# Where the tiles of a one-core decoder step lie in SBUF: normalised inputs every 2304 bytes, gated outputs every 2112, two places for raw weights

## The chip, the core and the metric

The program runs on one core of one Trainium2 chip. Five engines work side by side, each through a list of its own: TensorE (PE) multiplies, VectorE (DVE), ScalarE (ACT) and GpSimd (POOL) work element by element, and SyncE (SP) issues the DMAs. The metric is the device time of the whole program in microseconds, the median of several runs.

## What is computed

One step of a small decoder with two layers, for a prompt of 512 tokens and 8 single sample tokens; the 520 columns are kept side by side.

```python
def trunk(x, p, pos, hgrn_state, k_past, v_past, ...):
    for l in range(DEPTH):                      # DEPTH = 2
        xn = rmsnorm(h, pre_norm_g[l])
        if l < N_A_LAYERS:                      # layer 0: HGRN2
            mix, S = hgrn2_mixer(xn, w_in_a[l], lb_all[l], onorm_a[l], w_out_a[l], S0)
        else:                                   # layer 1: sliding-window attention with sinks
            kv = rmsnorm(h, kv_norm_g) @ w_kv
            ...
            u = xn @ w_in_b[j]
            q, z = jnp.split(u, 2, axis=-1)
            ...
            mix = (o.reshape(B, L, MIX_WIDTH) * jax.nn.silu(z)) @ w_out_b[j]
        h = h + rmsnorm(mix, post_norm_g[l])
        h = h + (p[l] @ w_pe[l]) * jax.nn.sigmoid(h @ w_pg[l])
```

Model width 1024, mixer width 2048, 16 heads of 128 in layer 0, 32 query heads of 64 over 4 key heads in layer 1, a window of 128. Everything is float32.

## The kernel before, in words

**Products in three passes.** Each float32 operand of a projection is split into a high and a low part that TensorE takes as fp32r. A product is hi·hi + lo·hi + hi·lo: `mm` (line 597) issues, for one weight chunk of 128 x 128 and one input tile, wh with x's high part, wl with x's high part, and wh with x's low part. Each pass is made for both halves of the 520 columns, 260 wide (`half_of`, line 411), so six matmuls of 260 columns for a chunk. Stages that are worked in halves of the sequence (`end_of`, line 419: the residual, the gates, the last output product) use 256 and 264 columns instead, from columns 0 and 256. The halves of one output go to a pair of PSUM banks, `pj`, of which there are two; other work uses single banks, `ph`.

**Weights.** `piece` (line 564) loads a weight tile of 128 x 1024 (512 KB) from HBM into one of three places `wr`. `halves` (line 585) makes from each half of it, a piece of 512 columns, the high part `wh` with an ACT cast and the low part `wl` with a subtraction on DVE or POOL. There are four places (`SPLITS`) for `wh` and four for `wl`, and every second pair of the gates' weights uses four pieces of the shared tag `b4`. A piece serves four chunks, 24 matmuls. `stream` (line 533) walks over all output tiles of the kernel in order and asks for a piece as soon as the one four pieces earlier has had its last use.

**Tiles of activations.** `act` (line 437) takes a place of 128 partitions by 520 float32 columns, 2080 bytes in each partition, from a pool in which each tag has a fixed number of places one behind the other. The tags lie in the order tmp, g, x, acc, og, xr, R, xs, behind the constants and the pool of wr, wh and wl; further pools follow behind xs. `xs_` (line 449) hands out the sixteen places of normalised inputs: high and low parts of eight row blocks, the moving operand of nearly all projections, and the gated outputs of the last heads. `og_` (line 452) hands out twelve places: the gated outputs of the other heads, which the output product reads, and before and between the layers some inputs and residuals.

**Order.** Nothing is issued where it is written. Each call is entered into a `Plan` with its dependencies; `issue` (line 209) then goes through a model of the engines, with a price for each instruction and a number of free places for each tag, and gives each engine its order. Where a tile's place isn't free in the model, its first writer isn't chosen; a DMA stands in SP's list by the same rule. SP's list is one queue for all DMAs: weights, states, turns of tiles through DRAM (`td`), results. At run time each engine keeps to its order and waits for semaphores.

**Stages.** Up to about 40 us the start: embedding products and the first head's projections from unnormalised inputs in og and xr. Then 15 more heads of layer 0, each with four projections of eight chunks, with the heads' own work beside them, and output products in groups. From about 570 to 635 us the second half of layer 0 (residual, gates). Then keys and values, eight units of layer 1 with four projections each, and from about 1010 us the last residual and gates.

All instructions are issued by one helper, so each has line 171 in the profile; the groups are told apart by their tiles' names.

Of the kernel before, what the change touches and what calls it, by code (L numbers as in the profile page):

```python
# [9 lines left out]
F32 = mybir.dt.float32  # L10
# [8 lines left out]
P = 128  # L19
D_MODEL = 1024  # L20
KC = D_MODEL // P
SEQ = 512
NB = 8
T = SEQ + NB
# [34 lines left out]
IDLE, SLOW = 3.4, 6.8  # L59

WINDOW, LOADS = 1600, 700

KEEP = {"tmp": 2, "g": 8, "xr": 4}

# [301 lines left out]
def bank_of(ps, h):  # L366
    return ps[h] if isinstance(ps, list) else ps[:, h]


def chunks_of(loads, n):  # L370

    ws = [Weights(loads[j]) for j in range(n)]
    return [(ws[m * n // KC], m * n % KC) for m in range(KC)]
# [45 lines left out]
def end_of(x, half):  # L419
    return x[:, ENDS[half][0] : sum(ENDS[half])]  # L420


class Step:
# [13 lines left out]
    def act(self, tag, bufs, dtype=F32, cols=T):  # L437
        return self.plan.tile(self.ap, [P, cols], dtype, self.name(tag), tag, bufs)

    def x_(self, dtype=F32):  # L440
        return self.act("x", 8, dtype)

# [4 lines left out]
        return self.act("g", 15, dtype, cols)  # L447

    def xs_(self, dtype=F32R):
        return self.act("xs", 16, dtype)  # L450

    def og_(self, dtype=F32R):
        return self.act("og", 12, dtype)

    def tmp_(self, dtype=F32, cols=T):
        return self.act("tmp", 4, dtype, cols)
# [107 lines left out]
    def piece(self, order, n):  # L564
        w, half = order[n]
        if half in w.pieces:
            return
        if w.raw is None or n < 2:

            cols = [half] if n < 2 else [h for h in range(2) if (w, h) in order]  # L570
            w.raw = self.plan.tile(self.wp, [P, KC * P], F32, self.name("wr"), "wr", 3)
            sl = slice(cols[0] * PIECE, (cols[-1] + 1) * PIECE)
            self.nc.sync.dma_start(w.raw[:, sl], w.src[:, sl])
        w.pieces[half] = self.halves(w.raw[:, half * PIECE : (half + 1) * PIECE], w.spare)
# [174 lines left out]
    def out_tiles(self, src, n, parts, before, mix, first, after=None):  # L749

        nc = self.nc
        xs = []

        def start():
            assert before()
            if not xs:
                xs.extend(parts())

        def evac(m):
            def f(ps):  # L760
                if first:
                    mix[m] = self.x_()
                    nc.scalar.copy(self.two(mix[m]), self.flat(ps))
                else:
                    nc.vector.tensor_tensor(self.two(mix[m]), self.two(mix[m]), self.flat(ps), op=ALU.add)

            return f

        def evac_half(q, half):
            def f(ps):  # L770
                for a in range(2):
                    m = 2 * q + a
                    x = end_of(mix[m], half)
                    nc.vector.tensor_tensor(x, x, bank_of(ps, a)[:, : ENDS[half][1]], op=ALU.add)
                    if m == 0 and half == 0:
                        self.acc = self.act("acc", 1)
                    self.square_into(end_of(self.acc, half), x, m == 0)
                if m == KC - 1:
                    after(half)

            return f

        at = chunks_of(src, n)
        if after is None:
            return [Tile128([at[m]], n, xs, evac(m), start) for m in range(KC)]
        return [
            Tile128(at[2 * q : 2 * q + 2], n, xs, evac_half(q, half), start, half)
            for half in range(2)
            for q in range(KC // 2)
        ]  # L790
# [615 lines left out]
    def pre_norm(self, xs, gain, raw, Rs, out):  # L1406

        nc = self.nc
        acc = self.act("acc", 1)
        for c in range(KC):  # L1410
            self.square_into(acc, xs[c], c == 0)
            g = self.vec[:, gain + c : gain + c + 1]
            hi, lo = self.og_(), self.og_() if c < 4 else self.xr_(F32R)
            nc.scalar.activation(hi, xs[c], AF.Copy, scale=g)
            nc.vector.scalar_tensor_tensor(lo, xs[c], g, hi.bitcast(F32), op0=ALU.mult, op1=ALU.subtract)
            raw.append((hi, lo))
        R = self.act("R", 1)
        for half in range(2):
            self.rstd(acc, half, R)
        Rs.append(R)  # L1420
        for c in range(KC):
            nc.vector.scalar_tensor_tensor(
                xs[c], xs[c], self.vec[:, gain + c : gain + c + 1], R, op0=ALU.mult, op1=ALU.mult
            )
            out.append(self.split(xs[c], self.xs_))
# [23 lines left out]
    def run(self):  # L1449
# [78 lines left out]
        def finish0(m, half, h):  # L1528
            if half == 0:
                if m == 0:  # L1530
                    self.acc1 = self.act("acc", 1)

                    both = self.small("m", [P, 2, T], 1)
                    self.C, self.S = both[:, 0], both[:, 1]
                    for t, src in ((self.C, "ropeC"), (self.S, "ropeS")):
                        nc.sync.dma_start(t, i[src])
                kvx.append((self.g_(F32R), self.og_()))
            self.beside(lambda: parts(m, half, h), SIDE if half == 0 and m < 4 else MAIN)

        def parts(m, half, h):  # L1540
            nc.sync.dma_start(end_of(hd[m], half), h)
            g = self.vec[:, KVG + m : KVG + m + 1]
            hi, lo = (end_of(x, half) for x in kvx[m])
            nc.scalar.activation(hi, h, AF.Copy, scale=g)
            nc.vector.scalar_tensor_tensor(lo, h, g, hi.bitcast(F32), op0=ALU.mult, op1=ALU.subtract)
            self.square_into(end_of(self.acc1, half), h, m == 0)
            if m == KC - 1:
                self.beside(lambda: self.kv_norm(half, h1, qx), FIRST)

        tiles += in_turn(end + self.gates(0, h1, h1x, pe[0], kept[0], finish0))  # L1550


# [182 lines left out]
```

## Time and profile before

| | us |
|---|---|
| median of 3 runs | 1081.44 |
| lowest and highest run | 1079.11, 1082.64 |
| span of the profiled execution, first to last instruction | 1076.6 |
| mean time between the span and the median of the runs | 4.8 |

The 4.8 us are the difference of two different executions; the profiled one's own time outside its span isn't shown. The memory traffic of the whole span is moderate, and the shortest transfers are the many of turned tiles:

```profile
HBM read 134.16 MB, written 31.97 MB: 154 GB/s over the span
```

In the rows of groups, the first number behind the bar is the group's busy time in us, the second the mean time of one instruction in ns, and then comes the idle time of the engine just ahead of them and who ended it. In rows of a timeline the first number is the start and the second how long the merged instructions took, both in us.

### The profile page before, as it was taken

The numbers are of one execution on the slowest core, as the hardware profiler recorded it, in microseconds if no ns is written. First come the engines' busy times: TensorE is split into PE (matmuls) and PEld (weight loads), VectorE is DVE, ScalarE is ACT, GpSimd is POOL, SyncE is SP. The second block draws the span as 40 slices with busy tenths as digits, with TensorE's granted clock in tenths as the row PEclk, the third lists the DMA queues.
The fourth block names the chain that finished last, engine by engine and source line by source line (L and its number), as shares of the span: only waits on it lengthen the run. The fifth ranks groups of instructions, "written<-read, shape, count | busy, mean of one in ns | idle before, by whom it ended". The sixth has DMA issues, their size and how long they took to land.

```text
span 1076.6 us, 24015 instructions
## 1 busy us (share of the span) xinstructions
PE 1064.7 (99%) x8876; PEld 1056.3 (98%) x8876; DVE 916.3 (85%) x1974; ACT 688.0 (64%) x1829; POOL 116.3 (11%) x196
## 2 busy tenths in 40 slices
PE   9999999999999999999999999999999999999998
PEld 8999999999999999999999999999999999999998
DVE  8897888884878968888889999799998988889984
ACT  7787777755777637767736565477677664665542
POOL 1121122101111012011110000000100001010000
PEclk9999999999999999999999999999999999999999
DMA  8455566655755657576654455644434253424432
GB/s 318 156 192 191 149 192 211 208 175 159 224 164 165 198 143 226 174 218 197 192 170 143 143 189 143 167 132 124 127 100 126 81 153 99 133 93 138 140 99 80
DMA packets 134397, 173.22 MB, mean 161 GB/s; under 512 B 69892, under 2 KB 88268, under 8 KB 134280
## 3 DMA queue, kind: packets, MB, share of 16 engines
q1 hardware_dynamic: 134280, 171.69, 52.1%
q8 instruction: 70, 1.15, 0.5%
q14 instruction: 47, 0.39, 0.1%
HBM read 134.16 MB, written 31.97 MB: 154 GB/s over the span
## 4 chain that ended last, share of the span: by engine, by line
PE 90%; DVE 4%; ACT 3%; issue 2%; DMA 1%; SPq 0%; POOL 0%; POOLq 0%; DVEq 0%; ACTq 0%
PE pj L171 69%; PE ph L171 21%; DMA xr<-td 1%; DVE tmp L171 1%; DVE wl L171 1%; DVE g L171 1%; ACT g L171 0%; ACT tmp L171 0%; ACT wh L171 0%; DVE x L171 0%; DVE xr L171 0%; ACT L171 0%; DVE xs L171 0%; SPq L171 0%; ACT sb L171 0%
## 5 line engine op out<-in xcount | busy, mean ns | idle before, releaser
L171 PE MATMUL pj<-xs,wh 128*128 128x260 f32 (+2 forms) x3264 | 558.7, 285 | 2.4 <-ACT xs L171 1.8
L171 PEld LDWEIGHTS pj<-xs,wh 128*128 128x128 f32 x3264 | 459.0, 188 | 4.3 <-ACT xs L171 3.0
L171 PE MATMUL pj<-xs,wl 128*128 128x260 f32 (+2 forms) x1632 | 338.8, 285 | 0.0
L171 PEld LDWEIGHTS pj<-xs,wl 128*128 128x128 f32 x1632 | 254.3, 188 | 0.2
L171 ACT CAST wh<-wr 128x512 fp32r<-128x512 f32 x288 | 177.5, 620 | 104.9 <-PE pj L171 90.8
L171 DVE TENSOR_TENSOR wl<-wr,wh 128x512 fp32r<-128x512 f32 x273 | 187.7, 690 | 44.2 <-ACT wh L171 40.6
L171 PE MATMUL pj<-og,wh 128*128 128x260 f32 x1056 | 183.3, 285 | 0.0
L171 PEld LDWEIGHTS pj<-og,wh 128*128 128x128 f32 x1056 | 149.7, 188 | 0.4 <-DVE g L171 0.2
L171 PE MATMUL pj<-og,wl 128*128 128x260 f32 x512 | 107.1, 286 | 0.0
L171 PEld LDWEIGHTS pj<-og,wl 128*128 128x128 f32 x512 | 80.1, 188 | 0.0
L171 ACT ACTIVATE tmp<-pj 128x520 f32<-128x520 f32 (+2 forms) x78 | 42.5, 556 | 49.8 <-PE pj L171 49.5
L171 ACT ACTIVATE sb<-sb,g 128x128 f32<-128x128 f32 x128 | 64.7, 560 | 5.1 <-DVE sb L171 5.1
L171 ACT ACTIVATE sb<-sb,nv 128x128 f32<-128x128 f32 x128 | 64.5, 565 | 0.4
L171 ACT COPY b<-ph 128x256 f32<-128x256 f32 (+1 forms) x80 | 27.7, 351 | 44.6 <-PE ph L171 44.1
L171 ACT ACTIVATE b<-b,an 128x129 f32<-128x129 f32 x128 | 50.7, 399 | 5.5 <-DVE an L171 4.5
L171 ACT COPY b<-g 128x256 f32<-128x256 f32 (+1 forms) x112 | 40.8, 375 | 20.7 <-DVE g L171 15.8
L171 PE MATMUL ph<-xs,b 128*128 128x256 f32 (+1 forms) x360 | 50.9, 283 | 0.0
L171 DVE TENSOR_TENSOR x<-x,pj 128x520 f32<-128x520 f32 (+2 forms) x64 | 39.6, 624 | 12.7 <-PE pj L171 12.3
L171 DVE COPY_PREDICATED xr<-lmask,ph 128x256 f32<-128x256 int32 x96 | 46.8, 489 | 3.3 <-PE ph L171 2.7
L171 PE MATMUL ph<-xr,b 128*128 128x128 f32 x320 | 49.1, 275 | 0.0
L171 DVE TENSOR_TENSOR g<-g,b 128x256 f32<-128x256 f32 x96 | 41.1, 429 | 8.1 <-PE ph L171 4.9
L171 PEld LDWEIGHTS ph<-xs,b 128*128 128x128 f32 x360 | 46.4, 188 | 0.1
(214 smaller groups left out, 1746.2 us busy)
## 6 DMA issues: line engine op xcount, KB each, us to landing
wr<-in_w_in_a SPq DMA_DIRECT2D x64, 512.0 KB, 4.8
sb<-sd SPq DMA_DIRECT2D x32, 512.0 KB, 4.7
wr<-in_w_in_b SPq DMA_DIRECT2D x32, 512.0 KB, 3.9
td<-tmp SPq DMA_DIRECT2D x42, 256.0 KB, 3.0
xr<-td SPq DMA_DIRECT2D x168, 64.0 KB, 3.6
sb<-in_state SPq DMA_DIRECT2D x16, 512.0 KB, 5.9
out_st_s<-sb SPq DMA_DIRECT2D x16, 512.0 KB, 2.9
wr<-in_w_out_a SPq DMA_DIRECT2D x16, 512.0 KB, 4.9
```

The costliest lines, as they stand in the source:

```text
L171: op = Op(len(self.ops), self.level, on, [lambda c=c: c(*a, **k) for c in calls], [self.price(e, name, ins, a, k) for e in on], on[0] == " ...
```

## The change

The sixteen xs places become 576 columns (2304 bytes) wide and the twelve og places 528 (2112 bytes); both hand out the 520 columns that begin four columns (16 bytes) into the place. The single place `acc` becomes 528 columns wide, of which the first 520 are used. Raw weights have two places `wr` instead of three. No instruction is added or removed, and no operand changes its shape.

```diff
+INSET, OG_COLS, XS_COLS = 4, T + 8, T + 56
...
+    def inset(self, tag, bufs, dtype, cols):
+
+        return self.act(tag, bufs, dtype, cols)[:, INSET : INSET + T]
+
...
     def xs_(self, dtype=F32R):
-        return self.act("xs", 16, dtype)
+        return self.inset("xs", 16, dtype, XS_COLS)

     def og_(self, dtype=F32R):
-        return self.act("og", 12, dtype)
+        return self.inset("og", 12, dtype, OG_COLS)
...
-            w.raw = self.plan.tile(self.wp, [P, KC * P], F32, self.name("wr"), "wr", 3)
+            w.raw = self.plan.tile(self.wp, [P, KC * P], F32, self.name("wr"), "wr", 2)
...
-                        self.acc = self.act("acc", 1)
+                        self.acc = self.act("acc", 1, cols=OG_COLS)[:, :T]
```

The same edit of `acc` stands in `pre_norm` (line 1409) and in `finish0` (line 1531). T is 520, P 128 and KC 8.

More of the change, by code (lines that the diff above doesn't have):

```diff
@@ L1408, in pre_norm @@
         nc = self.nc
-        acc = self.act("acc", 1)
+        acc = self.act("acc", 1, cols=OG_COLS)[:, :T]
         for c in range(KC):
@@ L1530, in finish0 @@
                 if m == 0:
-                    self.acc1 = self.act("acc", 1)
+                    self.acc1 = self.act("acc", 1, cols=OG_COLS)[:, :T]
                     both = self.small("m", [P, 2, T], 1)
```

## The prediction

> **What bounds the kernel now.** I read the page's table of busy times first, then its slices, then the chain of work that ended last, and last the groups kept apart by shape.
>
> ```profile
> PE 1064.7 (99%) x8876; PEld 1056.3 (98%) x8876; DVE 916.3 (85%) x1974; ACT 688.0 (64%) x1829; POOL 116.3 (11%) x196
> PEclk9999999999999999999999999999999999999999
> PE 90%; DVE 4%; ACT 3%; issue 2%; DMA 1%; SPq 0%; POOL 0%; POOLq 0%; DVEq 0%; ACTq 0%
> PE pj L171 69%; PE ph L171 21%; DMA xr<-td 1%; DVE tmp L171 1%; DVE wl L171 1%; DVE g L171 1%; ACT g L171 0%; ACT tmp L171 0%; ACT wh L171 0%; DVE x L171 0%; DVE xr L171 0%; ACT L171 0%; DVE xs L171 0%; SPq L171 0%; ACT sb L171 0%
> L171 PE MATMUL pj<-xs,wh 128*128 128x260 f32 x2944 | 500.2, 285 | 0.7 <-DVE xs L171 0.4 <-ACT xs L171 0.2
> L171 PE MATMUL pj<-xs,wl 128*128 128x260 f32 x1472 | 306.0, 285 | 0.0
> L171 PE MATMUL pj<-og,wh 128*128 128x260 f32 x1056 | 183.3, 285 | 0.0
> L171 PE MATMUL pj<-og,wl 128*128 128x260 f32 x512 | 107.1, 286 | 0.0
> ```
>
> TensorE is busy for 1064.7 of 1076.6 us at its full granted clock, and 90% of the chain is matmuls. Hardly anything ever waits in front of PE: 0.7 us of idle time stand before the 2944 commonest matmuls. So the kernel lasts as long as its list of matmuls, and only two things move the end much: how far apart consecutive matmuls start, or new gaps in the list.
>
> The mean of 285 ns is the time from a matmul's start to its end. Several are in flight, so it is not the pace. The pace is the distance from start to start. It can be read in the chain in order of time, where one unbroken run of projections stands:
>
> ```profile
> 657.81 33.86 PE pj L171 x283
> ```
>
> 33.86 us over 283 matmuls is 119.6 ns each. Multiplied by the 8876 records, 120 ns gives 1065 us, the busy time. The 260-wide products of xs (2944 + 1472 = 4416) and og (1056 + 512 = 1568) are two thirds of the list.
>
> **The pace and where an operand begins.** The change alters no instruction on PE; it alters the byte at which the moving operand begins. The program of before puts its first xs place at byte 153312 of a partition, which is 224 modulo 256, and the places are 2080 bytes (520 columns of four) apart. 2080 is 32 more than a multiple of 256, so the sixteen places go through all eight multiples of 32. A projection reads the second half at column 260, 1040 bytes on, 16 more modulo 256. The weight pieces wh and wl all begin at 160 modulo 256, before and after.
>
> I took the distance from each 260-wide xs matmul to the next 260-wide one, leaving out distances over 140 ns (gaps and changes of type), and sorted them by the starting byte modulo 256. The first and the last rows of the 4416:
>
> ```profile
> 41.44 0.41 PE L171 MATMUL pj<-xs,wh 128*128 128x260 f32 x2
> ...
> 961.78 0.40 PE L171 MATMUL pj<-xs,wh 128*128 128x260 f32 x2
> ```
>
> 4037 distances are left, with a mean of 119.8 ns. Two of the sixteen starts stand out: 144 (202 distances) with 117.9 ns and 160 (300) with 117.7 ns, each uncertain by 0.2. The other fourteen lie between 119.3 and 121.0, the slowest being 0, 64, 176 and 192 with 120.8 to 121.0. On og, whose places have other addresses, 144 gives 118.9 and 160 gives 118.3 against a mean of 119.8. So this isn't one tile's accident: the same two residues are quick in tiles far apart.
>
> The Trainium skill, "TensorE: Matmul & The Clock Gate", section "Wait — 56ns, not 53.3ns?", puts a warm matmul at its columns over 2.4 GHz plus about 2.5 ns; that would be 110.8 ns for 260 columns. The trace has 119.8, so some 9 ns of each matmul are not in that rule, which is room for a loss that depends on addresses.
>
> **The change part by part.**
>
> *xs places at 144.* Taking a wr place away moves what follows by −4096; the longer acc adds 32 and the longer og twelve times 32. 153312 − 4096 + 32 + 384 = 149632, which is 128 modulo 256, and four columns of inset make it 144. At a distance of 2304 = 9 × 256 all sixteen start at 144, so their second halves start at 160. The pace becomes (117.9 + 117.7) / 2 = 117.8 ns instead of 119.8: 2.0 ns by 4416 is **−8.7 us**. From below, nothing is gained if the two are quick for another reason (a rival); from above, both at the quicker of the two, 117.7, would be −9.3 us.
>
> *xs read from columns 0 and 256.* The stages of the gates (256 and 264 wide, 576 matmuls) now start both halves at 144. In that shape the trace shows no clear difference between residues, so 0, with ±1 ns or ±0.6 us as bounds.
>
> *og places at 16, 80, 144 and 208.* By the same sum og begins at 149632 − 12 × 2112 − 9 × 2080 = 105568 less R's 2080, that is 103488, 64 modulo 256, and 80 with the inset; 2112 is 64 more than a multiple of 256. Second halves start at 32, 96, 160 and 224. The eight xs means of these starts average 119.2: 0.5 ns by 1568 is **−0.8 us**, between 0 and −1.6.
>
> *ACT and DVE.* They write the same elements 16 bytes further on. Nothing is added to their lists. Before, second halves of 260 columns were already touched at 16 modulo 32, so I take 0; with DVE at 85% a loss of some per cent on the few hundred og and xs writes would be hidden under PE.
>
> *Two places for raw weights.* Each wr place holds 512 KB from HBM until ACT has cast both halves and DVE or POOL has subtracted. A load can start only when a place is free, so with two it starts one weight later.
>
> ```profile
> wr<-in_w_in_a SPq DMA_DIRECT2D x64, 512.0 KB, 4.8
> wr<-in_w_in_b SPq DMA_DIRECT2D x32, 512.0 KB, 3.9
> ```
>
> ```profile
> L171 ACT CAST wh<-wr 128x512 fp32r<-128x512 f32 x288 | 177.5, 620 | 104.9 <-PE pj L171 90.8 <-issue 7.7 <-DMA wr<-in_w_pe 2.5
> ```
>
> ```profile
> SPq L171 <- DVE wl L171: 165.1, 57, 10.0
> SPq L171 <- DVE xr L171: 61.0, 31, 10.4
> ```
>
> Of the 104.9 us that ACT idles before casts, 90.8 are ended by PE, which frees a wh place, and hardly any by the load. Here is one load in order of time:
>
> ```profile
> 305.90 0.68 DVE L171 TENSOR_TENSOR wl<-wr,wh 128x512 fp32r<-128x512 f32 x1
> 306.62 0.33 SPq L171 DMA_DIRECT2D wr<-in_w_in_a  x1
> 309.67 0.62 ACT L171 CAST wh<-wr 128x512 fp32r<-128x512 f32 x1 [3.13 <-PE pj L171]
> ...
> 313.92 0.69 DVE L171 TENSOR_TENSOR wl<-wr,wh 128x512 fp32r<-128x512 f32 x1 [0.99 <-PE ph L171]
> ...
> 323.52 0.62 ACT L171 CAST wh<-wr 128x512 fp32r<-128x512 f32 x1
> ```
>
> The load issued at 306.62 goes out the moment the subtraction three weights back ends (306.58), and is cast at 323.52. With two places it waits for the subtraction that ends at 314.61; 4.8 us later, at 319.4, it has landed, still 4.1 us before its cast. Behind the longer-waiting load stand SP's other DMAs, the turns through td among them, but the planner orders SP's list by the same places, so I expect the load to stand later in the list, not to hold it. Where there is no such cover is the start and the last gates:
>
> ```profile
> 1050.86 1.28 DVE L171 TENSOR_TENSOR wl<-wr,wh 128x512 fp32r<-128x512 f32 x2
> 1051.57 0.36 SPq L171 DMA_DIRECT2D wr<-in_w_pg  x1
> 1055.85 2.29 PE L171 MATMUL ph<-xs,b 128*128 128x256 f32 x18
> 1056.59 1.14 ACT L171 CAST b<-wr 128x512 fp32r<-128x512 f32 x2
> ```
>
> ```profile
> wr<-in_w_pg SPq DMA_DIRECT2D x16, 512.0 KB, 3.6
> ```
>
> The pair of gate weights used at 1055.85 would both be loaded after 1051.5 instead of one. 1051.6 + 3.6 for the load, 0.6 for a cast and 0.7 for a subtraction is 1056.5: 0.7 us late, if PE has nothing else. I take **+1 us** for all the places together, between 0 and +3 (the start, the gates of layer 0 and those of layer 1 at a microsecond each).
>
> *The order.* The planner writes every engine's order from modelled times and places. It doesn't know addresses, but fewer wr places shift its order a little. PE's idle time is 1076.6 − 1064.7 = 11.9 us; an estimate is that a quarter of it, 3 us, comes or goes.
>
> *The sum.* −8.7 − 0.8 = −9.5. PE is 90% of the chain, and what the other engines end isn't shortened by a quicker PE, so I count nine tenths, −8.6; with +1 that is **−7.6 us**. The profiled execution's span goes from 1076.6 to about 1069.0. The median of the runs, 1081.44, lies 4.8 us above that span, time around the first and the last instruction which the change doesn't touch. So the forecast is 1081.4 − 7.6 = **1073.8 us**, and 1069 to 1079 with its own bounds. The next limit is then again PE's list; DVE at 916 us is far from it.
>
> **The rivals.**
>
> *The pace stays.* In the trace 144 is always a second half that follows a start at 128, and 160 always a first half that a start at 176 follows; 144 and 160 never alternate. The quick pace may belong to those neighbours. Then only the wr place counts: 1081.4 + 1 = 1082.4 us. For it speaks that starts and neighbours can't be told apart by these rows; against it, that two residues side by side, in both roles and in several tiles, are the quick ones. The Trainium skill speaks for this rival: "SBUF — State Buffer", section "Who interferes with whom", says that PE never waits for anyone on its SBUF ports, and the section "Specifications (TRN2)" gives 16-byte lines, of which 1040 bytes from any multiple of 16 touch the same number, so by these rules the start would not matter. The spread of 117.7 to 121.0 in this trace is against them.
>
> *Half of it.* One of the two residues keeps its pace in its new role, the other doesn't: half of −8.6, so 1081.4 − 4.3 + 1 = 1078.1 us.
>
> *Weights come late: slower.* SP works in order, and its longest waits in the rows above are 10.0 and 10.4 us. A load that stands behind such a wait lands some 10.4 − 4.1 = 6.3 us after its cast's turn. ACT and its queue then stand still, and the evacuations of pj behind the cast; two pieces already split, at 24 matmuls by 120 ns each, cover 5.8 us. That leaves 0.5 us for each such case, with 24 heads and units 12 us: 1073.8 + 12 = 1086 us. It decides once loads commonly land more than about 4 us late. Against it: the load of the example has 4.1 us to spare, and where SP was held up before, the load was late already.
>
> *It doesn't land on 144.* If a tile in between is laid out otherwise, all sixteen places share another start. The worst pair, 192 and 208 with 121.0 and 119.9, costs 0.7 ns by 4416: 1082.4 + 2.9 = 1085 us.
>
> **How the numbers follow.** Forecast 0.58, half 0.10, pace stays 0.17, weights late 0.12, other start 0.03. A measurement of this kernel can tell about 0.3%, 3.2 us, from no change. Faster: nearly all of the forecast, half of "half": 0.62. Slower: weights late, another start, a quarter of "pace stays": 0.18. Same: 0.20. The range reaches from 1067 (the upper bound of the pace and 3 us of good order) to 1084, past "pace stays" and short of "weights late", which with the odd start leaves some 0.17 out.
>
> **What would show it.** The run of projections between units should read 117.8 ns a matmul instead of 119.6, and PE's busy time should fall by about 9 us with the same 8876 records. DVE's and ACT's means (690 ns for wl, 620 for wh) should not move. ACT's idle time before casts should still be ended by PE; if "DMA wr" takes its place, weights are late. If PE's busy time falls but the span doesn't, gaps ate the gain. The prediction fails if the pace stays at 119.8, or if the idle time of PE grows past 20 us.

## The result, and the profile after

The changed kernel took 1084.9 us (median of 7 runs, 1083.3 to 1087.94), the kernel before 1082.02 us beside it. The medians are 2.9 us apart; the ratio of the runs is 1.0041 with a 95% interval of 1.0027 to 1.0055, which is 4.4 us of 1080. So the kernel became slower by some 3 to 4 us, where 1073.8 us had been forecast. The profiled execution of the changed kernel has a span of 1085.4 us and took 1087.17 us; so 1.8 us lie outside the span, and not the 4.8 us that the table ahead of the prediction got from two different executions. The profiled execution of before was then one of the quick ones (1076.6 + 1.8 = 1078.4 us), and the 8.8 us between the two spans are two to three times what the runs show.

The page after, in the order in which the page before was read: busy times, granted clock, chain, groups by shape.

```profile
PE 1067.0 (98%) x8876; PEld 1057.1 (97%) x8876; DVE 915.2 (84%) x1970; ACT 688.5 (63%) x1829; POOL 117.7 (11%) x200
PEclk9999999999999999999999999999999999999999
PE 80%; DVE 9%; DMA 5%; ACT 2%; issue 2%; SPq 1%; POOL 1%; DVEq 0%; ACTq 0%; POOLq 0%
L173 PE MATMUL pj<-xs,wh 128*128 128x260 f32 x2944 | 502.8, 285 | 0.6 <-DVE g L173 0.6
L173 PE MATMUL pj<-xs,wl 128*128 128x260 f32 x1472 | 304.9, 285 | 0.0
L173 PE MATMUL pj<-og,wh 128*128 128x260 f32 x1056 | 185.6, 285 | 0.4 <-ACT wh L173 0.4
```

PE's busy time did not fall by 9 us, it rose by 2.3. Its idle time went from 11.9 us to 1085.4 − 1067.0 = 18.4 us. The chain, 90% matmuls before, is now 80% matmuls, with 9% DVE and 5% DMA. So two things happened: nothing became quicker, and new gaps opened.

I also added up every start-to-start distance on PE over 250 ns, less 120 ns each for the matmul itself: 26 such gaps with 11.1 us before, 37 with 19.3 us after. That is 8.2 of the 8.8 us between the spans. Shorter lapses (140 to 250 ns) add up, counted alike, to 26.0 us before and 26.4 us after, and all the rest to 993.3 and 991.6 us. Most of these lapses are no loss at all. They stand behind a change from fp32 to fp32r products, and there the distance just ahead is as much too short. Here is one such change before: two fp32 records, one fp32r product, then fp32 again:

```profile
141.72 0.38 PE L171 MATMUL ph<-b,xr 128*128 128x128 f32 x2
141.86 0.37 PE L171 MATMUL pj<-xs,wh 128*128 128x260 f32 x1
142.06 0.61 PE L171 MATMUL ph<-xr,b 128*128 128x128 f32 x4
```

From 141.72 to 142.06 us three matmuls start, 0.34 us or some 115 ns each, although the last of these distances, from 141.86 to 142.06, is a lapse of 0.2 us. Over all such changes the median distances are 31 ns into the fp32r product and 204 ns behind it, together 234 ns for two.

*The pace.* The unbroken run of projections that the prediction read in the chain of before stands in the chain of after too:

```profile
661.50 33.57 PE pj L173 x280
```

33.57 / 280 is 119.9 ns; before it was 119.6, and 117.8 had been forecast. All 260-wide xs matmuls after, first and last row:

```profile
43.76 0.40 PE L173 MATMUL pj<-xs,wh 128*128 128x260 f32 x2
...
970.37 0.40 PE L173 MATMUL pj<-xs,wh 128*128 128x260 f32 x2
```

Of their distances of at most 140 ns, 4035 are left. From a start at 144 to one at 160 it is 119.2 ns, from 160 to 144 it is 120.5, and the mean of all is 119.9 (before 119.8).

*The gaps.* The largest opens at 813.4 us. PE's timeline and then DVE's and POOL's just ahead of it (start, duration; the square bracket is the idle time before and who ended it):

```profile
813.09 0.64 PE L173 MATMUL pj<-xs,wh 128*128 128x260 f32 x4
815.47 0.63 PE L173 MATMUL ph<-ident,b 128*128 128x128 f32 x4 [1.74 <-DVE b L173]
```

```profile
799.59 1.33 DVE L173 SCALAR_TENSOR_TENSOR bg<-bo,zb 128x8 f32<-128x8 f32 x2
...
810.70 1.27 DVE L173 TENSOR_TENSOR og<-bg,og 128x8 fp32r<-128x8 f32 x1
```

```profile
799.02 1.80 POOL L173 TENSOR_TENSOR wl<-wr,wh 128x512 fp32r<-128x512 f32 x1 [16.15 <-DVE og L173]
803.72 1.50 POOL L173 TENSOR_TENSOR wl<-wr,wh 128x512 fp32r<-128x512 f32 x1 [2.90 <-ACT wh L173]
807.20 1.30 POOL L173 TENSOR_TENSOR wl<-wr,wh 128x512 fp32r<-128x512 f32 x1 [1.97 <-ACT wh L173]
810.16 1.78 POOL L173 TENSOR_TENSOR wl<-wr,wh 128x512 fp32r<-128x512 f32 x1 [1.67 <-ACT wh L173]
```

Busy times of PE, PE's weight loads, DVE, ACT and POOL in the stretch of 800 to 816 us, before and after:

```profile
800.00:816.00 16.00, 16.00 (x135) 15.87 (x134) 15.70 (x36) 10.80 (x32) 1.72 (x2) 1.00 0.56 157
```

```profile
800.00:816.00 16.00, 14.26 (x121) 14.08 (x120) 15.85 (x39) 11.09 (x39) 5.40 (x4) 1.00 0.39 111
```

DVE is full in both. Before, PE is busy for all 16 us beside it; after, PE runs out of other products and waits for `b`, which DVE makes. In between stand tiny instructions of 8 columns that take over a microsecond beside a subtraction on POOL, where others of the same kind take some 0.2 us for two. Another gap, 0.96 us from start to start, follows at 826.2. Where the same output's product starts in both traces, the changed kernel is some 3 us late around 400 us, some 2 us around 460 to 490, 3.7 us around 570 and again from 640 to 690, some 6 us at 800, 10.2 us at 830 and some 8 us from 910 to the end: the delay comes in several places, and the largest single gap is this one.

*The weights.* ACT's casts and DVE's subtractions among the groups, and SP's longest wait, after:

```profile
L173 ACT CAST wh<-wr 128x512 fp32r<-128x512 f32 x288 | 177.2, 619 | 117.2 <-PE pj L173 96.2 <-issue 10.1 <-DMA wr<-in_w_in_a 7.1
L173 DVE TENSOR_TENSOR wl<-wr,wh 128x512 fp32r<-128x512 f32 x272 | 186.2, 687 | 50.5 <-ACT wh L173 48.9
```

```profile
SPq L173 <- DVE wl L173: 199.2, 69, 9.8
```

Loads do wait more for a place (199.2 us instead of 165.1) and end 7.1 us of ACT's idle time where the row before names 2.5. Still PE ends most of the idle time ahead of casts, 96.2 of 117.2 us. PE itself now sometimes waits for weights: of the waits that its view of waits lists, 7.4 us before and 13.7 after, a part of a weight (wh, wl or the load behind them) ends none before and 3.2 us after. How much such late loads cost had to be tried.

### The profile page after: what moved, and what is told of

Same layout as the page of the kernel before. It is cut to its first block, busy times and chain, and to the rows that moved or that the text cites. A ratio compares the mean times of both kernels' runs of the same rounds, so it can differ in the third digit from the quotient of the medians.

```text
span 1085.4 us, 23989 instructions
## 1 busy us (share of the span) xinstructions
PE 1067.0 (98%) x8876; PEld 1057.1 (97%) x8876; DVE 915.2 (84%) x1970; ACT 688.5 (63%) x1829; POOL 117.7 (11%) x200
## 4 chain that ended last, share of the span: by engine, by line
PE 80%; DVE 9%; DMA 5%; ACT 2%; issue 2%; SPq 1%; POOL 1%; DVEq 0%; ACTq 0%; POOLq 0%
PE pj L173 62%; PE ph L173 18%; DVE tmp L173 2%; DMA xr<-td 2%; DVE g L173 1%; SPq L173 1%; DVE wl L173 1%; DVE b L173 1%; DVE og L173 1%; DVE ao L173 1%; DMA sinkb<-in_sinkb 1%; DMA pe<-g 1%; DVE xr L173 0%; DMA wr<-in_w_in_a 0%; DMA sb<-sd 0%
## 5 line engine op out<-in xcount | busy, mean ns | idle before, releaser
L173 ACT CAST wh<-wr 128x512 fp32r<-128x512 f32 x288 | 177.2, 619 | 117.2 <-PE pj L173 96.2
L173 PE MATMUL pj<-og,wh 128*128 128x260 f32 x1056 | 185.6, 285 | 0.4 <-ACT wh L173 0.4
L173 DVE TENSOR_TENSOR xr<-xr,b 128x256 f32<-128x256 f32 x96 | 40.9, 426 | 5.1 <-PE ph L173 3.5
```

The lines of the kernel that those rows point to most:

```text
L173: op = Op(len(self.ops), self.level, on, [lambda c=c: c(*a, **k) for c in calls], [self.price(e, name, ins, a, k) for e in on], on[0] == " ...
```

## The experiments

All ratios are to the kernel before, run beside each on the same chip, with 95% intervals. "Idle" is the span less PE's busy time of the page, from one profiled execution each. e4 has work added and is not in the table.

| kernel | places wr, as planned / real | layout | ratio | PE idle, us |
|---|---|---|---|---|
| before | 3 / 3 | old | 1 | 11.9 |
| changed | 2 / 2 | new | 1.0041 [1.0027, 1.0055] | 18.4 |
| e1 | 2 / 2 | old | 1.0058 [1.0041, 1.0074] | 18.0 |
| e2 | 2 / 3 | old | 1.0062 [1.0043, 1.0080] | 16.9 |
| e3 (changed) | 2 / 2 | new | 1.0038 [1.0023, 1.0052] | 16.0 |
| e5 | 2, then 3 / 3 | old | 1.0057 [1.0039, 1.0075] | 17.0 |
| e6 | 3, then 2 / 3 | old | 1.0007 [0.9989, 1.0025] | 13.8 |
| e7 | 3 / 3, other order | old | 1.0104 [1.0075, 1.0134] | 21.2 |
| e8 | 3 / 3 | xs, og every 2112 | 0.9978 [0.9964, 0.9992] | 11.8 |
| e9 | 3 / 3 | last pool moved | 1.0006 [0.9993, 1.0019] | 12.2 |
| e10 | 3 / 3 | as e8, last pool back | 0.9992 [0.9981, 1.0002] | 12.7 |
| e11 | 3 / 3, other order | old | 1.0003 [0.9989, 1.0016] | 13.5 |
| e12 | 3 / 3, other order | old | 1.0017 [1.0002, 1.0032] | 13.8 |
| e13 | 2 / 2, DVE for POOL | new | 1.0050 [1.0032, 1.0067] | 15.1 |
| e14 | 2 / 2 | xs, og every 2112 | 1.0059 [1.0043, 1.0074] | 16.7 |
| e15 (e8) | 3 / 3 | xs, og every 2112 | 0.9986 [0.9970, 1.0002] | 12.6 |
| e16 | 2 / 2, other order | new | 1.0036 [1.0025, 1.0047] | 17.0 |
| e17 | 2 / 2, other order | new | 1.0051 [1.0031, 1.0072] | 16.7 |
| e18 | 2 / 2, other order | new | 1.0046 [1.0027, 1.0066] | 16.6 |

**The pace by itself (e4).** The kernel before with a tail of 40 runs of 48 matmuls, whose moving operand begins at another residue in each run; nothing else is going on then. The tail comes on top of the computation, so its total time is not compared.

```diff
+        for step, at, starts in ((TH, 0, range(0, 64, 4)), (SEQ // 2, 0, range(0, 64, 4)), (TH, 16, range(0, 64, 8))):
+            for s in starts:
+                ps = self.pair()
+                for n in range(48):
+                    c = n // 2 % 3
+                    a = s + n % 2 * step
+                    nc.tensor.matmul(
+                        ps[:, n % 2, :TH], w[:, at + c * P : at + (c + 1) * P], big[:, a : a + TH],
+                        start=n < 2, stop=n > 45,
+                    )
```

> The kernel before, and behind it 40 runs of 48 matmuls of 260 columns with nothing beside them: 16 starts modulo 256 with the second operand 1040 bytes on, the same 16 with it 1024 bytes on, and 8 with the weights 64 bytes further. If the start sets the pace (the forecast's theory), the run at 144 and 160 takes 117.8 ns a matmul and the others 119.3 to 121, 1.4% and more apart. If a start only moves a matmul's beginning and the next gives it back (theory C), all 40 take the same time within 0.3 ns a matmul, though the distances inside a run alternate. If other engines' traffic makes the 9 ns over 110.8, the quiet runs come down towards 111.

```profile
1079.31 232.58 PE L171 MATMUL pj<-b,wh 128*128 128x260 f32 x1920 [2.64 <-ACT wh L171]
```

The run that goes back and forth between 144 and 160 takes 119.96 ns a matmul (first to last start, over 47), where the forecast's theory had 117.8. Inside it the distances alternate between 118.96 and 121.00 ns. So a start shifts when a matmul begins, and the next one gives it back; a distance sorted by one start is not a pace.

Theory C isn't met to the letter either, for it wanted all runs within 0.3 ns. The first run holds the start-up. Of the other fifteen of the first set twelve lie between 119.2 and 120.4 ns; 118.2 (starts at 176 and 192), 123.3 (112 and 128) and 123.0 (16 and 32) stand apart. The 24 runs of the other two sets lie between 119.1 and 121.7. The starts at 176, 112 and 16 alone don't make the outliers: with the second operand 1024 bytes on, their runs have 120.6, 119.9 and 120.0 ns. Nor does the pair: in the og products of the changed kernel the distances from 16 to 32 and from 32 to 16 average 118.8 and 119.6. Each outlier was seen once, and its cause is open.

The 9 ns above 110.8, the prediction's estimate from the Trainium skill, are not a cost of other engines' traffic: they are there in quiet too.

**The places, and the order that comes with them (e1, e2).** e1 is the kernel before with two places and the old layout. e2 keeps three places, and only the planner counts with two, so that every list is ordered as in e1 while a load has one place more at run time.

```diff
-            w.raw = self.plan.tile(self.wp, [P, KC * P], F32, self.name("wr"), "wr", 3)
+            w.raw = self.plan.tile(self.wp, [P, KC * P], F32, self.name("wr"), "wr", 2)
```

> Two places for raw weights, all tiles laid out as before; every engine's order is the changed kernel's. If the two places make the change slow (theory A), the time is that of the changed kernel, 1.003 to 1.006 of before. If the new layout makes it slow (theory B), it is within 0.2% of before. If the layout brings what was forecast and the places cost more than that, it is slower than the changed kernel, 1.010 or more.

```diff
             w.raw = self.plan.tile(self.wp, [P, KC * P], F32, self.name("wr"), "wr", 3)
+            self.plan.homes[w.raw.tensor.name] = "wr", 2
```

> The planner reckons with two places, so the order is the changed kernel's, but three places are there; layout of before. If loads that really come late cost the time (A1), the gaps of PE at the start and around 813 us shrink and the time is within 0.2% of before. If the changed order alone costs it (A2), it stays at 1.003 to 1.006.

e1 took 1086.03 us, e2 1086.28. The longest waits of SP in e2, as the view of waits lists them:

```profile
SPq L171 <- DVE g L171: 113.8, 31, 11.7
...
SPq L171 <- DVE wl L171: 49.9, 16, 9.9
```

With a third real place SP's waits for `wl` fall from 197.2 us in e1 to 49.9, and no time comes back. SP waits longer for other things instead, 113.8 us for `g` where e1 has 75.5. The gap ahead of `b` is there as well:

```profile
814.32 0.63 PE L171 MATMUL ph<-ident,b 128*128 128x128 f32 x4 [1.64 <-DVE b L171]
```

So the missing place itself is not the cost; the order that the planner writes for two places is, SP's list of loads included. That order is no small shift: 5498 of PE's 8440 instructions stand elsewhere than before, the same ones in the changed kernel, e1 and e2. Weights do come late in it now and then, and a third real place doesn't cure that: parts of a weight end 2.6 us of PE's waits in e1 and 2.2 in e2. This is the smaller part of what PE waits for. The fourth corner, two real places in the order for three, was not tried.

**Which part of the order (e5, e6).** Three real places in both; the planner counts two in layer 0 and three from layer 1 on (e5), or the reverse (e6).

```diff
+                if low >= self.second and not more:
+                    more = True
+                    self.slots["wr"].free.insert(0, 0.0)
...
+            self.plan.homes[w.raw.tensor.name] = "wr", 2
```

> Three places are there, layout of before; the planner reckons with two until layer 0 is all issued, then with three. The order for two costs 0.6% as a whole. Theory D (the loss sits in particular stages, the largest step being that of 2 and 1 us gaps of PE at 812 and 825 us in layer 1): 1.002 to 1.003 here, with the steps at 332, 360 and 505 us, and no gap at 812. Theory E (any other order of this kernel is some tenths of a per cent slower): 1.003 to 1.008, with gaps in new places.

```diff
+                if low >= self.second and less is None:
+                    less = 1
...
+                    if less and homes[name] == "wr":
+                        less = 0
+                        continue
```

> Three places, layout of before; the planner reckons with three in layer 0 and with two from layer 1 on. Theory D: 1.003 to 1.004, with the gaps at 812 and 825 us, and nothing different before 620 us. Theory E: anything from 1.000 to 1.008, and the two halves do not add up to 1.006.

e5 has all the loss, 1.0057, and has gaps at 812, 819 and 824 us too, in layer 1, where its planner had three places; e6 stays near the kernel before, 1.0007. The gap at 813 us therefore doesn't come from a shortage of places at that point, as theory D had it; the order takes its course in layer 0. Theory E missed in one point, for the two halves add up within the noise: 0.57% and 0.07%, against 0.62% in e2.

**The layout (e3, e8, e9, e10).** e3 is the changed kernel again, for its comparison with e1, which has the same order. The other three have three places and on every engine the order of the kernel before: e8 with og and xs every 2112 bytes, e9 with only the pool behind xs moved by 160 bytes, e10 as e8 with that pool back at its old residue (`11 * P + 24`).

> The changed kernel itself, on the same chip as the other two: 1.003 to 1.006 of before by both theories; it is there to be compared with.

```diff
+INSET, OG_COLS, XS_COLS = 4, T + 8, T + 8
```

> Three places and the order of before, instruction for instruction; xs and og both every 2112 bytes with four columns of inset, so starts at 16, 80, 144 and 208. The changed kernel stood 0.2% below the kernel with two places and the old layout, in the same order. If that is the layout and odd multiples of 16 do it, 0.997 to 0.999 here; if it takes the single start of the full change, or if the 0.2% are nothing, 1.000 within 0.1%.

```diff
-        self.lmask = self.plan.tile(self.sp, [P, 11 * P], I32, "lmask", "m", 1)
+        self.lmask = self.plan.tile(self.sp, [P, 11 * P + 40], I32, "lmask", "m", 1)
```

> Three places and order of before, xs and og as before; only the tag m is 160 bytes longer, so that every later tile of the last pool (the b tiles: states, spare weights, chunks) lies 160 bytes further and b4 begins at 224 modulo 256 instead of 64, as in the part-layout kernel. In that kernel ACT's strided activations on the state tiles sb were 3 to 6 ns shorter and TensorE's pace was the same. If the 0.2% come with the b tiles (theory F), 0.997 to 0.999 here; if they come with xs and og (theory G), 1.000 within 0.1%.

> The part-layout kernel with the tag m 96 bytes longer, so that the b tiles lie at their old residues (b4 at 64) again; xs and og every 2112 bytes with inset. Theory F: 1.000 within 0.1%, ACT's activations on sb as long as before. Theory G: 0.997 to 0.999.

e3 gave 1083.87 us against 1086.03 of e1, and e8 1078.51 us, 0.22% below the kernel before. But the two parts of e8, each by itself, gave 1.0006 and 0.9992, which is no difference that these runs can tell. The layout is worth between nothing and 0.2%.

**Other orders (e7, e11, e12).** The kernel before with one constant of the planner changed, and so another order: HAND 0.3 to 0.31, the price of a DMA 3.3e5 to 3.2e5, the latency behind DVE 0.20 to 0.21.

```diff
-HAND = 0.3
+HAND = 0.31
```

> Layout and three places of before; only the planner's constant HAND is 0.31 instead of 0.30, which puts 5193 of PE's 8440 instructions elsewhere in its list. If two places make a bad order (theory D), an order that has nothing to do with places stays within 0.2% of before. If the order of before is a lucky draw (theory E), this one is slower too, 1.002 to 1.008.

```diff
-            return aps[0].nbytes() / 3.3e5, False
+            return aps[0].nbytes() / 3.2e5, False
```

> Layout and three places of before; the planner prices a DMA's bytes 3% higher, which puts 3470 of PE's 8440 instructions elsewhere. If the order of before is a good draw among its neighbours (theory E), slower by 0.2 to 1.0%; if only fewer places or coarser turns on PE make it slower (theory D), 1.000 within 0.2%.

```diff
-LAT = {"tensor": 0.28, "vector": 0.2, "scalar": 0.25, "gpsimd": 0.17}
+LAT = {"tensor": 0.28, "vector": 0.21, "scalar": 0.25, "gpsimd": 0.17}
```

> The same with the planner's latency behind VectorE at 0.21 instead of 0.20 us, which moves 3394 of PE's instructions. Theory E: slower by 0.2 to 1.0%; theory D: 1.000 within 0.2%.

A third or more of PE's instructions stand elsewhere in each, and the ratios are 1.0104, 1.0003 and 1.0017. So an order isn't slower for being another one, but none of them was below the kernel before. e7 loses by gaps like the others: 44 distances over 250 ns with 23.0 us, against 26 with 11.1 before. It also goes from fp32 to fp32r products 547 times instead of 212 and has 676 short lapses (55.0 us) instead of 314 (26.0 us). But the distances under 100 ns, those just ahead of such lapses, fall short of 120 ns by 52.8 us in e7 and 20.5 us before. That gives the lapses back.

**POOL beside DVE (e13).** The changed kernel; the four subtractions of the fence above are issued on DVE at the same places of the program.

```diff
-            self.tc.keep_in_program_order(op.calls[n]())
+            self.tc.keep_in_program_order(op.calls[0 if op.n in (9775, 9802, 9840, 9867) else n]())
```

> The changed kernel with the planner's order as it is, but the four subtractions that POOL makes at 799 to 812 us go to DVE at the same places of the program. Theory P (POOL's long subtractions stretch DVE's short two-input instructions there, 1.33 and 1.27 us instead of some 0.2, and so make the gaps of PE at 813 and 826 us): the stretched ones fall back below 0.3 us, the two gaps (2.0 and 1.0 us) mostly close, and the time falls by 2 to 3 us, to a ratio of about 1.0015. Rival Q (the order itself asks too much of DVE between 796 and 830 us): four times 0.69 us more on DVE is no less than the 2.2 us it gains, the gaps stay or grow, and the ratio is 1.004 to 1.006.

The tiny instructions are short again, and nothing is won (DVE's timeline, PE's, and the busy times of the stretch):

```profile
795.48 0.24 DVE L173 SCALAR_TENSOR_TENSOR bg<-bo,zb 128x8 f32<-128x8 f32 x2
...
807.27 0.16 DVE L173 TENSOR_TENSOR og<-bg,og 128x8 fp32r<-128x8 f32 x1
```

```profile
811.54 0.63 PE L173 MATMUL ph<-ident,b 128*128 128x128 f32 x4 [1.91 <-DVE b L173]
```

```profile
800.00:816.00 16.00, 14.09 (x117) 13.82 (x116) 15.91 (x39) 12.29 (x45) 0.19 (x1) 1.00 0.38 113
```

DVE is as full as before (15.91 of 16 us), the gap ahead of `b` is no smaller (2.19 us from start to start, 2.03 in the changed kernel), and the ratio is 1.0050. The stretched instructions were real and not the cause, and theory P falls. Rival Q agrees with the run. That the order asks too much of DVE there is the reading that is left; it isn't shown by itself, since DVE is nearly as full before (15.70 of 16 us) without such a gap.

**The layout once more (e14, e15).** e14 is the changed kernel with xs every 2112 bytes instead of 2304 (`INSET, OG_COLS, XS_COLS = 4, T + 8, T + 8`) and with two places, e15 is e8 again.

> The changed kernel with xs every 2112 bytes as og, from 144 modulo 256 on in steps of 64, instead of all at 144; two places for raw weights, each engine's order as in the changed kernel. Theory L (the layout gives about 0.2% whatever the order, by moving where the tiles behind and the strided reads begin): 1.0035 to 1.004, that is 0.2% below the same order with the old layout (1.0058). Rival N (the layout gives nothing, and the differences of 0.2% seen so far are the spread of comparisons): 1.005 to 1.006. Were it the common start of all xs at 144 that helps, this kernel would lose that against the changed one, 1.004, and stand at the old layout's 1.0058 too.

> The kernel before with og and xs every 2112 bytes and three places for raw weights, each engine's order as in the kernel before: the one that stood below both kernels, 0.9978 [0.9964, 0.9992]. Theory L: 0.997 to 0.999 again, with an interval that leaves out 1. Rival N: 0.9995 to 1.001.

e14 shows nothing of a gain, 1.0059; e15 shows 0.9986, with an interval that just reaches 1. For e14 its expectation had named this outcome also for the case that the common start at 144 is what helps, which e14 lacks. The pace gives that little room: in this one order the close distances of the 260-wide xs matmuls average 119.97 ns in e1, 120.03 in e14 and 119.9 in e3 and the changed kernel, and 0.1 ns by 4416 is 0.4 us. Between "0.2%" and "nothing" these runs do not decide. e8 and e15 are one kernel, the only one that came out below the kernel before both times, with medians of 1078.51 and 1078.33 us beside 1080.96 and 1080.24; I would call its gain likely and not shown.

**Do two places cost the time in any order? (e16, e17, e18)** The changed kernel in three other orders: the price of a DMA as in e11, the latency as in e12, HAND 0.3 to 0.29.

> The changed kernel (new layout, two places for raw weights) with another order: the planner's price of a DMA from 3.3e5 to 3.2e5 bytes a microsecond; 2207 of PE's 8440 instructions stand elsewhere. Theory S (two places as such cost nothing, the order that the planner happened to write for them costs some 6 us): this order comes out anywhere between 0.998 and 1.010, as the other orders with three places did, and at least one of the three such kernels below 1.002. Rival T (planning with two places costs 4 to 6 us whatever the order): all three between 1.003 and 1.007 or above.

> The changed kernel with a third order: the planner's latency behind DVE from 0.20 to 0.21 us; 2997 of PE's instructions stand elsewhere. Theory S: between 0.998 and 1.010, one of the three below 1.002. Rival T: 1.003 to 1.007 or above.

> The changed kernel with a fourth order: the planner's constant HAND from 0.30 to 0.29 us; 3341 of PE's instructions stand elsewhere. Theory S: between 0.998 and 1.010, one of the three below 1.002. Rival T: 1.003 to 1.007 or above.

1.0036, 1.0051 and 1.0046: all three pay, none is below 1.002. The idle time of PE says the same. In the table every kernel whose layer 0 was planned with three places, e7 aside, has 11.8 to 13.8 us, and every one planned with two there has 15.1 to 18.4 us. Theory S, that the changed kernel had merely met a bad order, falls: four of four orders for two places lose 0.36 to 0.62%, and three of four for three places lose at most 0.17%. Still, e7, planned with three, lost most of all, so it isn't shown that every order for two places is worse than every order for three.

The planner knew. It ends with a modelled time of its own (`self.end`, the last line of `issue`), which is no device time and comes from its prices alone: 1063.8 us for before, 1068.0 for the changed kernel, e1 and e2, 1066.9 for e5, 1065.3 for e6, 1064.8 and 1065.2 for e11 and e12, 1069.4, 1068.7 and 1068.6 for e16 to e18, and 1072.5 for e7. The rise of 4.2 us from three places to two is close to the 4.4 us measured for the changed kernel, and less than the 6.3 of e1, whose order is the same. It is no measure of each kernel (e5 rises by 3.1 us and loses 6, e16 rises by 5.6 and loses 4), but the kernels with a rise of up to 1.5 us are those that lost at most 0.17%, and e7, with the largest rise, lost most. My reading is that in the model the missing place makes loads and the casts behind them start later, that the planner rearranges work around that, and that the chip then runs what was rearranged, whether a third place is there or not. That the chip's gap at 813 us is the same wait that the model saw was not traced.

## Why the prediction was wrong, step by step

**What bounds the kernel: right.** PE's list bounds both kernels, at the same clock, and "how far apart consecutive matmuls start, or new gaps in the list" were indeed the two things to look at. The gaps decided.

**The pace, −8.7 and −0.8 us: the step that failed.** "Two of the sixteen starts stand out" was read correctly from the trace and means something else. 117.9 and 117.7 ns were distances from such a start to whatever came next. A matmul at 144 or 160 is followed sooner, and another distance is longer for it; the mean of all, 119.8, was the pace. The prediction's own list shows a part of that: behind 160 with 117.7 ns stood 176, among the slowest with some 121. With all starts at 144 and 160 the two distances are 119.2 and 120.5, and e4 has 119.96 in quiet. The term of −8.7 us is gone: the mean went from 119.8 to 119.9 ns, and against e1, in the same order, it fell by 0.1 ns or 0.4 us. For og the mean stayed at 119.8 ns, so nothing came of the −0.8 us either. The prediction had seen the warning and set it too low: "144 and 160 never alternate" before, so their sum had never been measured. The rival "the pace stays", with a chance of 0.17, was right on this. So was the reading that it took from the Trainium skill ("SBUF — State Buffer", "Who interferes with whom" and "Specifications (TRN2)"), that the start would not matter: the traces agree within 0.1 ns for the means in the program, with three unexplained runs of 118.2 to 123.3 ns in e4 as exceptions.

**Two places, +1 us between 0 and +3: mis-sized, and in the wrong place.** The example load had 4.1 us to spare, and I priced how late loads would land. e1 measures the edit alone at +0.58%, 6.3 us (e16 to e18, with the new layout, stand at 0.36 to 0.51%); e2 shows that none of it needs the place to be missing at run time. "Weights come late", at 1086 us, came near to the measured 1084.9 by luck: it took 12 us for held-up loads and set them on 1073.8 us, a sum that already held the gain in pace which did not come. Weights end only 3.2 us of PE's waits in the changed kernel.

**The order, "an estimate is that a quarter of it, 3 us, comes or goes": the term that holds the loss.** It was put at zero because its sign seemed open, though the planner was given less to plan with, and all four orders for two places lose. "Fewer wr places shift its order a little" was wrong as well: 5498 of PE's 8440 instructions moved. PE's idle time was the right measure (11.9 to 18.4 us). Of the two signs in "the prediction fails if the pace stays at 119.8, or if the idle time of PE grows past 20 us" the first came, and the second was set too high: 18.4 us was enough.

**ACT and DVE unchanged: right.** wl 690 ns before and 687 after, wh 620 and 619. **The layout of the tiles: right as placed**, since xs starts at 144 and 160 only.

The sum with the measured terms: pace 0, two places +6.3 us with their order (e1), layout 0 to −2 us, together +4.3 to +6.3 us, against the +4.4 us that a ratio of 1.0041 makes of 1080. The layout's part comes from such ratios itself, so this sum is no independent test.

## What to carry to other kernels

A start-to-start distance sorted by a property of the first matmul is not a pace: what one gains, the next may give back, so add up the distances over a whole cycle, or try the combination that is wanted by itself. The same goes for a distance that looks like a lapse: see whether the one ahead of it is too short. Where a planner writes the order, a buffer taken away can be paid for in the order even if it is never missed at run time; plan for the smaller number and leave the buffer in place to tell the two apart. Such a planner's own modelled end, with and without the change, is worth a look beside the profile.

## What the runs showed of the hardware that had not been expected

- 260 columns of fp32r go at 119.1 to 121.7 ns in 36 of the 39 quiet runs of e4 behind the start-up, 119.96 for the pair of 144 and 160. So the 110.8 ns that the prediction estimated from the Trainium skill are not reached here even with all other engines idle. Why, no run shows; that PE's weight loads, one for each matmul and 97 to 98% busy in both pages, set the pace was not tried.
- Two-input DVE instructions of 8 columns took 1.33 us (two) and 1.27 us (one) beside a POOL subtraction of 1.8 us, and 0.24 us (two) and 0.16 us (one) when POOL was idle in e13. The POOL subtractions took 1.30 to 1.80 us in the changed kernel. The Trainium skill, "SBUF — State Buffer", section "Who interferes with whom", says that DVE and GpSimd share a pair of ports under an exclusive lock; these rows agree with it.
- A change from fp32 to fp32r products looks like a lapse and costs nothing to speak of. In 209 of the 212 changes before, the ones without a gap beside them, the first fp32r product starts 31 ns behind the last fp32 record (median) and the next 204 ns behind that, 234 ns in all, where two ordinary distances in these traces, 111 ns between fp32 records and 120 between fp32r products, are 231.
